# An encoder layer on one core: the first shift-and-scale block summed on TensorE, x and that block loaded first, sixteen feature tiles in six chunks

## The chip, the cores and the metric

One core of a Trainium2 chip runs the whole layer. The metric is device microseconds of one execution; a profiled execution is a separate one with its own time. The profile names five engines and their queues: PE (TensorE), PEld (its weight loads), DVE (VectorE), ACT (ScalarE), POOL (GpSimd), SP (the queue that issues nearly all loads here).

## What is computed

A residual block of width 2048 on 512 tokens. Before any matmul of the token mixer can run, its input `h` has to be normed and modulated by a shift and a scale that come out of a matrix-vector product with 4096 columns of `w_mod`:

```python
cond = jax.nn.silu(c)
mod = (cond @ w_mod[layer] + b_mod[layer]).astype(x.dtype)
shift_a, scale_a, gate_a, shift_m, scale_m, gate_m = [
    m[:, None, :] for m in jnp.split(mod, N_MOD, axis=-1)]
h = _rmsnorm(x, pre_mix_g[layer]) * (1.0 + scale_a) + shift_a
proj = h @ w_in[layer]
```

Attention, a bidirectional gated recurrence, the output projection and the MLP follow; the change touches none of them.

## The kernel before, in words

The 2048 features are 16 **feature tiles** of 128 (`kt`, 0 to 15). Every fp32 product of `h` and a weight is made of three matmuls (`mm3`, lines 227 to 230): high part by high part, and two cross terms. The high part `wH` of a weight chunk is cast on ACT (line 214), the low part `wL` subtracted on DVE (line 215).

The **front stage** (lines 572 to 650) makes `h` for all 16 tiles and, while it does, multiplies them by the four first groups of `w_in`. It takes the tiles in **chunks**, `bounds = [0, 2, 4, 8, 12, 16]`: tiles 0-1, 2-3, 4-7, 8-11, 12-15. For a chunk it needs:

1. the **block** of shift and scale columns of these tiles (`mod_block`, lines 249 to 278): row 16p + k of `w_mod` lies on partition p, and step k of 16 multiplies the block's columns by `cond[:, k]` on DVE and adds them into `modacc` (line 269 the first step, line 271 the other 15). The pieces arrive as tile `mraw`, 512 KB each, two steps of a two-tile block or one of a four-tile block. `to_cols` (lines 280 to 300) then sums over the partitions with one-column matmuls against `ones` on PE (line 295, `modc`), and three small DVE operations make the columns `hb` and `hs`. A block of two tiles has 512 columns, one of four 1024;
2. the transposed tile `xT` on PE (line 627 for the first chunk, by a diagonal of the norm factors; line 629 later), `hv` and `hH` on ACT (lines 631, 632), `hL` on POOL (line 633);
3. the weights: `start_block` (lines 388 to 404) multiplies groups `hg`, `qf`, `bi` in PSUM banks `shg`, `sqf`, `sbi`, four banks a group, two of which can be in use at once. In the first chunk ACT copies a finished bank (line 402), in every later one **DVE adds it** to what stands there (line 404), twelve adds a chunk. The fourth group, `res`, stays in four PSUM banks of its own through all chunks.

The blocks are worked one chunk ahead: `pers` says how many steps of the coming block go beside each weight chunk, `interleave` hands them out, `cuts` spreads the steps of the first block between the loads of `x` (line 594). A scheduler orders each engine's instructions by priority (`tc.high_priority(offset=...)`); each engine and the SP queue then run in that fixed order. `mraw` has four buffers, and a load waits on SP until its buffer is free.

Of the kernel before, what the change touches and what calls it, by code (L numbers as in the profile page):

```python
# [20 lines left out]
P = 128  # L21
S = 512
NT = S // P
# [29 lines left out]
def encoder_layer(ctx: ExitStack, tc: tile.TileContext, a, out):  # L53
# [195 lines left out]
    def mod_block(accs, spans, fin, own=None, pri=PRI):  # L249
# [11 lines left out]
        def step(c):  # L261
            def run():
                with tc.high_priority(offset=pri):
                    _, v = load(source(nk * c, nk), nk, w, own)
                    for k in range(nk):
                        kt = nk * c + k
                        if kt == 0:
                            st["acc"] = accs("modacc")
                            nc.vector.tensor_scalar(st["acc"][:, :w], v[:, k, :], cond[:, 0:1], None, ALU.mult)
                        else:  # L270
                            nc.vector.scalar_tensor_tensor(st["acc"][:, :w], v[:, k, :], cond[:, kt:kt + 1],  # L271
                                                           st["acc"][:, :w], ALU.mult, ALU.add)
            return run
# [6 lines left out]
    def to_cols(h_b, h_s, b_b, b_s, g, bank):  # L280
        def fin(acc):
            n = h_b.shape[-1]
            if n == 4 and bank is sdt:
# [36 lines left out]
    with ExitStack() as ph:  # L320
# [67 lines left out]
        def start_block(gid, k0, k1, units, per, tiles):  # L388
            pri = PRI if k0 else 0
# [182 lines left out]
        with pool("start", side="right") as stp:  # L572
# [3 lines left out]
            def mraw():  # L576
                return stp.tile([P, 1024], F32, tag="mraw", name="mraw", bufs=4)

            bounds = [0, 2, 4, 8, 12, 16]
            mod = []  # L580
            for i in range(len(bounds) - 1):
                k0, k1 = bounds[i], bounds[i + 1]
                w = (k1 - k0) * P
                ks = slice(k0, k1)
                mod.append(mod_block(acc_in(hg), [(P * k0, w), (2048 + P * k0, w)],
                                     to_cols(hb[:, ks], hs[:, ks], b_sa[:, ks], b_ca[:, ks], g_mix[:, ks], mmt), mraw,
                                     PRI if i else 0))
            ahead = [u for m in mod[1:] for u in m]
            pers = [3, 4, 2, 2, 0]
            cuts = [2, 3, 4, 6, 8]  # L590
            for u in mod[0][:cuts[0]]:
                u()
            for t in range(NT):
                nc.sync.dma_start(xn[:, t, :], x_d[t * P:(t + 1) * P, :])
# [23 lines left out]
            res = [banks["mm"].tile([P, 512], F32, tag="res", name=f"res{t}", bufs=4) for t in range(NT)]  # L618
            for i in range(len(bounds) - 1):
# [15 lines left out]
                for gid in order:  # L635
                    start_block(gid, k0, k1, ahead, per, tiles)
                for kt in range(k0, k1, 2):
# [702 lines left out]
```

## Time and profile before

| | us |
|---|---|
| runs of the kernel before | 2435.24, 2437.25, 2430.69 (median 2435.24) |
| the profiled execution's own time | 2436.67 |
| its span, first to last instruction | 2434.8 |
| PE busy, share of the span | 2345.1, 96% |
| DVE busy, share of the span | 1784.1, 73% |

The span is what the trace can be read against; 1.9 us of the execution lie outside it. The shares are means over the whole layer. The front stage is its first tenth and is read by itself, from the timeline and from windows of it; a bracket at the end of a timeline row is the idle time just before it and what ended it.

### The profile page before, as it was taken

The numbers are of one execution on the slowest core, as the hardware profiler recorded it, in microseconds if no ns is written. First come the engines' busy times: TensorE is split into PE (matmuls) and PEld (weight loads), VectorE is DVE, ScalarE is ACT, GpSimd is POOL, SyncE is SP. The second block draws the span as 40 slices with busy tenths as digits, with TensorE's granted clock in tenths as the row PEclk, the third lists the DMA queues.
The fourth block names the chain that finished last, engine by engine and source line by source line (L and its number), as shares of the span: only waits on it lengthen the run. The fifth ranks groups of instructions, "written<-read, shape, count | busy, mean of one in ns | idle before, by whom it ended". The sixth has DMA issues, their size and how long they took to land.

```text
span 2434.8 us, 29654 instructions
## 1 busy us (share of the span) xinstructions
PE 2345.1 (96%) x11342; PEld 1943.7 (80%) x11342; DVE 1784.1 (73%) x2222; ACT 932.9 (38%) x1439; POOL 120.9 (5%) x127
## 2 busy tenths in 40 slices
PE   4999999999999999999999999899999999999998
PEld 3778888888977777779888788778888888888886
DVE  6984776767867667487688888676786678677777
ACT  5223334343454432275533333333333233333342
POOL 0111212121110000000000000000000000000000
PEclk9999999999999999999999999999999999999999
DMA  9873353535531158475345354343333332333234
GB/s 316 288 243 96 113 174 96 173 98 176 184 89 35 35 173 264 150 251 182 121 151 168 114 185 143 107 121 96 118 95 104 92 119 88 109 95 113 87 119 132
DMA packets 193801, 341.77 MB, mean 140 GB/s; under 512 B 16886, under 2 KB 65148, under 8 KB 192124
## 3 DMA queue, kind: packets, MB, share of 16 engines
q1 hardware_dynamic: 192464, 339.72, 44.1%
q8 instruction: 89, 1.46, 0.2%
q14 instruction: 52, 0.43, 0.1%
q10 hardware_dynamic: 1196, 0.16, 0.1%
HBM read 331.45 MB, written 8.39 MB: 140 GB/s over the span
## 4 chain that ended last, share of the span: by engine, by line
PE 62%; DMA 4%; DVE 3%; ACT 1%; issue 1%; DVEq 0%; ACTq 0%; SPq 0%
PE up L230 9%; PE up L228 9%; PE up L229 9%; PE dn L1180 8%; PE dn L1182 8%; PE dn L1181 8%; DMA raw<-in_w_mod_dram 3%; PE wo L229 1%; PE wo L230 1%; PE wo L228 1%; DVE modacc L271 1%; PE upl L230 1%; PE upl L229 1%; PE upl L228 1%; DMA modbg<-in_b_mod_dram 1%; PE sc L880 1%
## 5 line engine op out<-in xcount | busy, mean ns | idle before, releaser
L233 ACT CAST wH<-B 128x1024 fp32r<-128x1024 f32 x210 | 221.2, 1053 | 508.6 <-PE up L229 198.2
L234 DVE TENSOR_TENSOR wL<-B,wH 128x1024 fp32r<-128x1024 f32 x210 | 256.5, 1222 | 175.9 <-PE dn L1181 65.0
L1180 PE MATMUL dn<-wH,fH 128*128 128x512 f32 x840 | 330.2, 393 | 9.2 <-DVE G L1046 7.7
L1182 PE MATMUL dn<-wH,fL 128*128 128x512 f32 x840 | 328.0, 390 | 0.0
L1181 PE MATMUL dn<-wL,fH 128*128 128x512 f32 x840 | 327.3, 390 | 0.0
L214 ACT CAST wH<-raw 128x512 fp32r<-128x512 f32 (+1 forms) x320 | 181.9, 612 | 360.2 <-PE wo L230 57.8
L215 DVE TENSOR_TENSOR wL<-raw,wH 128x512 fp32r<-128x512 f32 (+1 forms) x320 | 220.2, 721 | 91.4 <-issue 49.4
L271 DVE SCALAR_TENSOR_TENSOR modacc<-raw,cond,modacc 128x1024 f32<-128x1024 f32 x120 | 159.3, 1328 | 85.8 <-DMA raw<-in_w_mod_dram 85.1
L230 PE MATMUL up<-recH,wL 128*128 128x512 f32 (+1 forms) x544 | 207.9, 382 | 0.0
L228 PE MATMUL up<-recH,wH 128*128 128x512 f32 (+1 forms) x544 | 207.9, 382 | 0.0
L230 PE MATMUL up<-atH,wL 128*128 128x512 f32 (+1 forms) x544 | 204.6, 379 | 3.0 <-DVE wL L215 3.0
L229 PE MATMUL up<-recL,wH 128*128 128x512 f32 (+1 forms) x544 | 207.3, 381 | 0.0
L228 PE MATMUL up<-atH,wH 128*128 128x512 f32 (+1 forms) x544 | 205.5, 378 | 0.0
L229 PE MATMUL up<-atL,wH 128*128 128x512 f32 (+1 forms) x544 | 205.3, 378 | 0.0
L234 DVE TENSOR_TENSOR wL<-raw,wH 128x1024 fp32r<-128x1024 f32 x120 | 146.4, 1220 | 73.9 <-issue 46.5
L1180 PEld LDWEIGHTS dn<-wH,fH 128*128 128x128 f32 x840 | 158.0, 188 | 45.7 <-DVE G L1046 7.8
L233 ACT CAST wH<-raw 128x1024 fp32r<-128x1024 f32 x120 | 126.4, 1054 | 163.4 <-PE dn L1182 145.5
L1182 PEld LDWEIGHTS dn<-wH,fL 128*128 128x128 f32 x840 | 158.0, 188 | 34.7
L1181 PEld LDWEIGHTS dn<-wL,fH 128*128 128x128 f32 x840 | 158.2, 188 | 33.4 <-DVE B L1149 0.2
L1191 DVE TENSOR_TENSOR y<-y,dn 128x1024 f32<-128x1024 f32 x142 | 172.2, 1213 | 1.1 <-PE dn L1182 1.0
L230 PEld LDWEIGHTS up<-atH,wL 128*128 128x128 f32 x544 | 102.6, 190 | 22.2 <-DVE wL L215 3.2
L230 PEld LDWEIGHTS up<-recH,wL 128*128 128x128 f32 x544 | 102.0, 188 | 22.2
(369 smaller groups left out, 4665.9 us busy)
## 6 DMA issues: line engine op xcount, KB each, us to landing
raw<-in_w_up_dram SPq DMA_DIRECT2D x136, 512.0 KB, 3.8
raw<-in_w_mod_dram SPq DMA_DIRECT2D x128, 512.0 KB, 4.1
B<-in_w_down_dram SPq DMA_DIRECT2D x120, 512.0 KB, 4.2
raw<-in_w_in_dram SPq DMA_DIRECT2D x128, 256.0 KB, 3.1
mraw<-in_w_mod_dram SPq DMA_DIRECT2D x48, 512.0 KB, 5.1
raw<-in_w_out_dram SPq DMA_DIRECT2D x40, 512.0 KB, 4.3
raw<-in_w_in_dram SPq DMA_DIRECT2D x24, 512.0 KB, 5.0
mraw<-in_w_mod_dram SPq DMA_DIRECT2D x32, 256.0 KB, 3.9
```

Of the source, the lines that this page charges most:

```text
L214: nc.scalar.copy(H[:, o], raw[:, o])
L215: nc.vector.tensor_tensor(L[:, o], raw[:, o], H[:, o].bitcast(F32), ALU.subtract)
L228: nc.tensor.matmul(o, s_h, m_h, start=first, stop=False)
L229: nc.tensor.matmul(o, s_h, m_l, start=False, stop=False)
L230: nc.tensor.matmul(o, s_l, m_h, start=False, stop=last)
L233: nc.scalar.copy(h_out, src)
L234: nc.vector.tensor_tensor(l_out, src, h_out.bitcast(F32), ALU.subtract)
L271: nc.vector.scalar_tensor_tensor(st["acc"][:, :w], v[:, k, :], cond[:, kt:kt + 1], st["acc"][:, :w], ALU.mult, ALU.add)
L1180: nc.tensor.matmul(o, sh, mh, start=first, stop=False, skip_group_check=skip)
L1181: nc.tensor.matmul(o, sh, ml_, start=False, stop=False, skip_group_check=skip)
L1182: nc.tensor.matmul(o, sl, mh, start=False, stop=last, skip_group_check=skip)
L1191: nc.vector.tensor_tensor(dst, dst, Xv, ALU.add)
```

## The change

`mod_block` takes a `bank`: with one, every step is four one-column matmuls on PE that sum the pieces straight into a PSUM tile `modp`, and `to_cols` reads its sums there, without `modacc`, `ones` and line 295. Only the first block (`BY_PE = 1`) goes that way, in a bank of the `res` tag. Its loads and those of `x` get priority 400. `mraw` has six buffers for four, the chunk of tiles 4-7 becomes 4-5 and 6-7, `pers` and `cuts` follow, and the first chunk's weights get the priority of the others (`pri = PRI`).

```diff
--- before.py
+++ after.py
@@ -246,7 +246,7 @@
     def acc_in(p):
         return lambda name: p.tile([P, 1024], F32, tag="modacc", name=name, bufs=2)
 
-    def mod_block(accs, spans, fin, own=None, pri=PRI):
+    def mod_block(accs, spans, fin, own=None, pri=PRI, bank=None):
         st = {}
         w = sum(n for _, n in spans)
         nk = 1024 // w
@@ -262,9 +262,15 @@
             def run():
                 with tc.high_priority(offset=pri):
                     _, v = load(source(nk * c, nk), nk, w, own)
+                    if bank and c == 0:
+                        st["acc"] = bank("modp")
                     for k in range(nk):
                         kt = nk * c + k
-                        if kt == 0:
+                        if bank:
+                            for j in range(w // P):
+                                nc.tensor.matmul(st["acc"][:, j:j + 1], v[:, k, j * P:(j + 1) * P], cond[:, kt:kt + 1],
+                                                 start=kt == 0 and j == 0, stop=kt == KD - 1 and j == w // P - 1)
+                        elif kt == 0:
                             st["acc"] = accs("modacc")
                             nc.vector.tensor_scalar(st["acc"][:, :w], v[:, k, :], cond[:, 0:1], None, ALU.mult)
                         else:
@@ -280,7 +286,9 @@
     def to_cols(h_b, h_s, b_b, b_s, g, bank):
         def fin(acc):
             n = h_b.shape[-1]
-            if n == 4 and bank is sdt:
+            if bank is None:
+                sums = [acc[:, 0:n], acc[:, n:2 * n]]
+            elif n == 4 and bank is sdt:
                 sums = []
                 for o in (0, 4):
                     ps = bank("modt")
@@ -386,7 +394,7 @@
             return pss
 
         def start_block(gid, k0, k1, units, per, tiles):
-            pri = PRI if k0 else 0
+            pri = PRI
             hl_ = []
             for kt in range(k0, k1, 2):
                 pcs, w = group_pieces(gid, kt, 2)
@@ -574,24 +582,30 @@
             diag = stp.tile([P, NT, P], F32, name="diag")
             ss = small.tile([P, NT], F32, tag="ssl", name="ssx")
             def mraw():
-                return stp.tile([P, 1024], F32, tag="mraw", name="mraw", bufs=4)
-
-            bounds = [0, 2, 4, 8, 12, 16]
+                return stp.tile([P, 1024], F32, tag="mraw", name="mraw", bufs=6)
+
+            def rest(name):
+                return banks["mm"].tile([P, 512], F32, tag="res", name=name, bufs=4)
+
+            bounds = [0, 2, 4, 6, 8, 12, 16]
             mod = []
+            BY_PE = 1
             for i in range(len(bounds) - 1):
                 k0, k1 = bounds[i], bounds[i + 1]
                 w = (k1 - k0) * P
                 ks = slice(k0, k1)
                 mod.append(mod_block(acc_in(hg), [(P * k0, w), (2048 + P * k0, w)],
-                                     to_cols(hb[:, ks], hs[:, ks], b_sa[:, ks], b_ca[:, ks], g_mix[:, ks], mmt), mraw,
-                                     PRI if i else 0))
+                                     to_cols(hb[:, ks], hs[:, ks], b_sa[:, ks], b_ca[:, ks], g_mix[:, ks],
+                                             None if i < BY_PE else mmt), mraw,
+                                     PRI if i else 400, rest if i < BY_PE else None))
             ahead = [u for m in mod[1:] for u in m]
-            pers = [3, 4, 2, 2, 0]
-            cuts = [2, 3, 4, 6, 8]
+            pers = [3, 3, 3, 4, 3, 0]
+            cuts = [1, 2, 3, 4, 8]
             for u in mod[0][:cuts[0]]:
                 u()
             for t in range(NT):
-                nc.sync.dma_start(xn[:, t, :], x_d[t * P:(t + 1) * P, :])
+                with tc.high_priority(offset=400):
+                    nc.sync.dma_start(xn[:, t, :], x_d[t * P:(t + 1) * P, :])
                 for u in mod[0][cuts[t]:cuts[t + 1]]:
                     u()
             for u in mod[0][8:]:
@@ -615,7 +629,7 @@
             g1 = hg.tile([P, NT, 512], F32, tag="gate", name="gate", bufs=2)
             gt_t[1] = g1
             order = [("hg", 0), ("qf", 0), ("bi", 0)]
-            res = [banks["mm"].tile([P, 512], F32, tag="res", name=f"res{t}", bufs=4) for t in range(NT)]
+            res = []
             for i in range(len(bounds) - 1):
                 k0, k1 = bounds[i], bounds[i + 1]
                 with tc.high_priority(offset=PRI):
@@ -634,6 +648,7 @@
                 per = pers[i]
                 for gid in order:
                     start_block(gid, k0, k1, ahead, per, tiles)
+                res = res or [rest(f"res{t}") for t in range(NT)]
                 for kt in range(k0, k1, 2):
                     pcs, w = group_pieces(("hg", 1), kt, 2)
                     H, L = chunk(pcs, 2, w)
```

In the orders below a row is an instruction or a run of like ones (xN), in program order of its engine; the line numbers of the changed kernel are its own (271 is the new matmul, 275 and 277 the DVE steps, 412 the adds).

PE at the very start of the changed kernel (`modp` are the new sums, `xT` the transposed first tiles, `shg` the first weight group):

```order
L271 MATMUL modp_131<-cond_84,mraw_128 128x1 x2
L126 MATMUL ps_st1_109<-ident_73,st1_100 128x96
L641 MATMUL xT_247<-diag_126,xn_125 128x128
L641 MATMUL xT_256<-diag_126,xn_125 128x128
L641 MATMUL xT_247<-diag_126,xn_125 128x128
L641 MATMUL xT_256<-diag_126,xn_125 128x128
L271 MATMUL modp_131<-cond_84,mraw_128 128x1 x6
L271 MATMUL modp_131<-cond_84,mraw_141 128x1 x8
L271 MATMUL modp_131<-cond_84,mraw_153 128x1 x8
```

64 `modp` products stand on PE where the kernel before has 4 products of line 295; four products on `diag` stand ahead of all but the first two, and four more (not shown) behind the 48th.

DVE at the start, before:

```order
L269 TENSOR_SCALAR modacc<-mraw,cond 128x512
L271 SCALAR_TENSOR_TENSOR modacc<-mraw,cond,modacc 128x512 x5
L238 RECIPROCAL ssx<-ssx 128x2
L271 SCALAR_TENSOR_TENSOR modacc<-mraw,cond,modacc 128x512 x4
L238 RECIPROCAL ssx<-ssx 128x2
L271 SCALAR_TENSOR_TENSOR modacc<-mraw,cond,modacc 128x512 x6
L297 TENSOR_TENSOR hb<-modc,cols 128x2
L298 TENSOR_TENSOR hs<-modc,cols 128x2
L269 TENSOR_SCALAR modacc<-mraw,cond 128x512
```

and now:

```order
L238 RECIPROCAL ssx<-ssx 128x2 x2
L215 TENSOR_TENSOR wL<-raw,wH 128x512 x2
L305 TENSOR_TENSOR hb<-modp,cols 128x2
L306 TENSOR_TENSOR hs<-modp,cols 128x2
L307 SCALAR_TENSOR_TENSOR hs<-hs,cols 128x2
L275 TENSOR_SCALAR modacc<-mraw,cond 128x512
L277 SCALAR_TENSOR_TENSOR modacc<-mraw,cond,modacc 128x512 x5
```

The 16 DVE steps of the first block are gone; the first step of the second block stands behind the sums of the first in both.

DVE in the chunk of tiles 6-7 of the changed kernel (`gate`, `q`, `z`, `v` are the adds, 128x1024 the steps of the block of tiles 8-11):

```order
L277 SCALAR_TENSOR_TENSOR modacc<-mraw,cond,modacc 128x1024
L412 TENSOR_TENSOR gate<-gate,shg_1016 128x512
L412 TENSOR_TENSOR gate<-gate,shg_1024 128x512
L277 SCALAR_TENSOR_TENSOR modacc<-mraw,cond,modacc 128x1024
L412 TENSOR_TENSOR gate<-gate,shg_1032 128x512
L277 SCALAR_TENSOR_TENSOR modacc<-mraw,cond,modacc 128x1024
L412 TENSOR_TENSOR gate<-gate,shg_1040 128x512
L277 SCALAR_TENSOR_TENSOR modacc<-mraw,cond,modacc 128x1024
```

This chunk's adds are new as a set of twelve: before, tiles 4-7 shared one set.

## Rows read from the trace of the kernel before

**Rows 1.** Windows of DVE, columns: stretch, length, busy (count), granted clock, DMA, GB/s:

```profile
32.09:156.74 124.65, 111.18 (x130) 0.97 0.88 295
156.74:200.30 43.56, 25.20 (x36) 0.97 0.48 144
```

**Rows 2.** Timeline of the start, columns: start, duration, engine, line, operation, tiles:

```profile
6.75 1.91 ACT L601 ACTIVATE hL<-xn 128x2048 fp32r<-128x2048 f32 x1 [2.15 <-DMA xn<-in_x_dram]
...
13.09 1.91 ACT L601 ACTIVATE hL<-xn 128x2048 fp32r<-128x2048 f32 x1 [4.33 <-DMA xn<-in_x_dram]
...
17.00 0.69 ACT L606 ACTIVATE diag<-ident,ssx 128x128 f32<-128x128 f32 x2 [0.29 <-DVE ssx L238]
17.45 2.08 PE L627 MATMUL xT<-diag,xn 128*128 128x128 f32 x8 [9.58 <-ACT diag L606]
...
25.39 0.69 ACT L606 ACTIVATE diag<-ident,ssx 128x128 f32<-128x128 f32 x2 [0.23 <-DVE ssx L238]
...
30.04 1.87 PE L295 MATMUL modc<-ones,modacc 128*128 128x1 f32 x8 [2.12 <-DVE modacc L271]
...
32.09 0.48 DVE L269 TENSOR_SCALAR modacc<-mraw,cond 128x512 f32<-128x512 f32 x1
...
41.56 1.14 ACT L214 CAST wH<-raw 128x512 fp32r<-128x512 f32 x2 [6.36 <-DMA raw<-in_w_in_dram]
...
42.23 0.80 PE L228 MATMUL shg<-wH,hH 128*128 128x512 f32 x1 [6.70 <-ACT wH L214]
```

**Rows 3.** Timeline of weight loads and PE, passes at either clock level:

```profile
30.04 1.78 PEld L295 LDWEIGHTS modc<-ones,modacc 128*128 128x128 f32 x8 [2.42 <-DVE modacc L271]
...
45.09 0.63 PE L229 MATMUL shg<-wL,hH 128*128 128x512 f32 x1
45.52 0.63 PE L230 MATMUL shg<-wH,hL 128*128 128x512 f32 x1
...
47.09 0.39 PE L228 MATMUL shg<-wH,hH 128*128 128x512 f32 x1
47.32 0.39 PE L229 MATMUL shg<-wL,hH 128*128 128x512 f32 x1
...
88.73 1.84 PE L295 MATMUL modc<-ones,modacc 128*128 128x1 f32 x16
```

**Rows 4.** Timeline of DVE, the steps, the low parts and the adds:

```profile
25.30 4.69 DVE L271 SCALAR_TENSOR_TENSOR modacc<-mraw,cond,modacc 128x512 f32<-128x512 f32 x6
...
47.56 1.29 DVE L215 TENSOR_TENSOR wL<-raw,wH 128x512 fp32r<-128x512 f32 x2 [0.33 <-ACT wH L214]
...
66.70 2.59 DVE L271 SCALAR_TENSOR_TENSOR modacc<-mraw,cond,modacc 128x1024 f32<-128x1024 f32 x2
...
70.19 1.28 DVE L271 SCALAR_TENSOR_TENSOR modacc<-mraw,cond,modacc 128x1024 f32<-128x1024 f32 x1
71.38 0.68 DVE L404 TENSOR_TENSOR gate<-gate,shg 128x512 f32<-128x512 f32 x1
...
76.82 1.28 DVE L404 TENSOR_TENSOR q<-q,sqf 128x512 f32<-128x512 f32 x2
```

**Rows 5.** Who DVE waited for between 32.09 and 156.74, columns: us in total, times, longest:

```profile
DVE hb L297 <- PE modc L295: 3.7, 3, 2.0
DVE gate L404 <- PE shg L230: 2.8, 3, 1.7
```

**Rows 6.** Timeline around the first bank of tiles 8-11 and of tiles 12-15:

```profile
155.08 0.50 PE L229 MATMUL shg<-wL,hH 128*128 128x512 f32 x1 [2.84 <-DVE wL L215]
...
156.74 0.68 DVE L404 TENSOR_TENSOR gate<-gate,shg 128x512 f32<-128x512 f32 x1
...
160.86 0.69 DVE L404 TENSOR_TENSOR gate<-gate,shg 128x512 f32<-128x512 f32 x1 [2.25 <-PE shg L230]
...
202.82 0.39 PE L228 MATMUL shg<-wH,hH 128*128 128x512 f32 x1
```

**Rows 7.** Window of PE from its first weight matmul, columns as in rows 1:

```profile
42.23:156.74 114.51, 106.47 (x517) 0.97 0.88 296
```

## The prediction

> **What bounds the kernel now.** The page's engine shares (table above) come first: PE is busy 96% of the span, so outside the front stage time moves only with PE's own work, which is the same in both kernels from the last chunk of tiles on. The question is when that chunk starts. Its first matmul stands at 202.82 us [rows 6].
>
> The windows of DVE come next. From 32.09, its first step for the second block, to 156.74, its first add for tiles 8-11, DVE is busy 111.18 of 124.65 us; from there to 200.3 it is busy 25.20 of 43.56 [rows 1]. So up to 156.74 DVE carries nearly all of the time, and after it PE does. I call 156.74 the **milestone**: DVE works in program order, so every step, low part and add ahead of that add has to be done first, and PE can be at most two banks ahead of it. PE's wait just before it, 2.84 us, is for a low part of DVE [rows 6].
>
> The start is read from the timeline [rows 2]. The second pair of norm diagonals is there at 25.39, the sums of the first block begin on PE at 30.04, DVE is free for the second block at 32.09; the first weight matmul starts only at 42.23 because its weights were loaded behind pieces of the second block (cast at 41.56, after 6.36 us of waiting for the load).
>
> **The change, part by part.**
>
> *x first.* x now stands behind one piece of the block instead of between many. The second quarter of x had 3.4 MB loaded up to its end and was used at 13.09; the first had 1.3 MB and was used at 6.75 [rows 2]. It now has 2.36 MB, so by a straight line about 9.9. From the second square to the first diagonal took 3.9 us (13.09 to 17.00): 13.8 now; the second diagonal stands behind one more square (1.91 and its read-out of 0.19), 16.2. Nothing of this is on the path by itself. It matters because PE's order puts four diagonal products ahead of the 3rd `modp` product, so the sums really begin at about 17.3.
>
> *Block one on PE.* A product is two passes in the trace: the four of line 295 show as x8. Eight passes took 1.87 us at 30.04, sixteen took 1.84 us at 88.73 [rows 3], so 0.47 us a product at the lower clock level (1.2 GHz) and 0.23 at the higher (2.4). That it is the lower at 30.04 is told by the 512-column passes: they start every 0.43 us at 45.09 and every 0.23 at 47.09 [rows 3]; the record of the granted clock only begins at 47. A one-column product is nearly all weight load: eight loads took 1.78 of the 1.87 us [rows 3]. (The Trainium skill, "TensorE: Matmul & The Clock Gate", section "LDWEIGHTS (loading the stationary operand)", gives a load columns divided by 1.2 in ns, so 0.107 us for 128 whatever the columns moved; as an estimate the 128 loads would cost 13.7 us. The row has 0.22 for each of these fp32 loads, twice that, and it decides; on the point that a single moved column pays for a whole load the trace agrees.)
>
> 64 products cost 30 us at the lower level, 15 at the higher. PE idles for most of the time before 42.23, so nobody has seen whether a run of such products raises the clock. I take that it rises after some 4.5 us of unbroken work, as it did between 42.23 and 47 [rows 2, 3]: 4.5 us from 17.3 do 10 of the 46 products ahead of the next diagonal pair, 36 more take 8.4, four diagonal products 1.0 (half of 2.08 [rows 2]), the last 16 take 3.7. That ends at 34.9, with `hb` out at 35.1 and DVE free for block two at **35.3 against 32.09, 3.2 us later**. The end not taken is the first rival's, 48.8. What went away, 16 DVE steps of 0.78 us (six in 4.69 [rows 4]), lay where DVE was waiting for loads, and frees nothing later, because block two still stands behind the sums in DVE's order.
>
> *First matmul.* `hH` follows `hs` by some 2 us, as before, and the weights are already cast. The first weight matmul comes at about 37.3 instead of 42.23. That is 5 us gained on PE. It is only kept if PE is the bound, and by rows 1 it is not.
>
> *Six chunks.* I counted DVE's operations from the start of block two to the milestone in both orders. Steps of 512 columns: 45 for 15, at 0.78: +23.4. Steps of 1024: 27 for 39, at 1.25 (1.30 each where two follow one another, 1.19 to the start of the next operation where an add follows [rows 4]): -15.0. First steps of a block, three of 512 and two of 1024 for one and three: +0.2. Adds: 36 for 24, two in 1.28 [rows 4]: +7.7. Low parts: 34 for 36, two in 1.29: -1.3. That is +15.0. Two thirds of the new 512-steps alternate with other work, where a 1024-step was 0.11 us cheaper; this takes off 2: **+13.0**, between 11 and 15. Part of it, three steps, is work for tiles 12-15 done earlier than before; that helps nobody, as PE bounds afterwards.
>
> *DVE's idle time.* 13.5 us lay idle before the milestone [rows 1], most of it waits for PE: 3.7 for the sums of a block and 2.8 for `gate` banks lead the list [rows 5]. With more to do and PE ahead of it, DVE waits less. I leave 4.5 us: waits for the four block sums (one of them was up to 2.0 us [rows 5]) and for the weights of the first chunk. **-9.0**; the ends are -13.5 and -4.
>
> *Behind the milestone.* Before, PE had finished one bank of tiles 8-11 at 156.74; the second add came at 160.86, 2.25 us of it waited for [rows 6]. From the milestone to the last chunk's first matmul it took 46.1 us. When DVE is late, PE stands two banks ahead: twelve passes, 2.7 us less. **-2.5**.
>
> *Six mraw buffers, priorities, pers, cuts.* Priced at nothing by themselves. The DMA share up to the milestone is 0.88 [rows 1], and in the changed order loads wait for DVE to free `mraw`, so more buffers can't go faster than DVE. If that cover were gone, loads would bound instead, at 295 GB/s: the 45 MB of x, weights and pieces ahead of the milestone need 153 us, still under the time DVE needs.
>
> **Sum.** 3.2 + 13.0 - 9.0 - 2.5 = +4.7 us on 2436.67, the profiled execution: 2441.4. The runs shown have a median of 2435.24, 1.4 lower, which would give 2440; I write **2441**. With the ends of the terms this case runs from 2431 to 2450. A measurement of this kernel can tell about 0.3%, 7.3 us, from no change.
>
> **The rivals.**
>
> *The sums stay at the lower clock level.* For it: every short burst on PE before 42.23 ran at that level, and a one-column product moves almost nothing. Against: PE works without a break from 17.3 on, which none of those bursts did. Then 46 products take 21.5, four diagonals 2.1, sixteen 7.5: the sums end at 48.4 and DVE begins block two at 48.8, 16.7 us late. DVE idles 2 us less, loads having run ahead. 16.7 + 13.0 - 11.0 - 2.5 = +16.2: 2452 to 2453, clearly slower, and the first matmul comes at about 50.
>
> *DVE does keep up, and the time falls.* The price is PE's: 5 us at the start, and what of 8.0 us idle (114.51 less 106.47 [rows 7]) and some 4 us at the lower clock up to the milestone goes. Up to -17, 2420. It decides if DVE's work per two-tile chunk stays under PE's 23 us (96 passes of 0.23 and the transposes). Sixteen steps of 0.7 to 0.78, eight low parts of 0.64 and twelve adds of 0.64 make 24 to 25 us before any disturbance, and 32 in the chunk of tiles 6-7, whose sixteen steps are of 1024 columns. That speaks against it; smoother chunks and less lockstep speak for it.
>
> *The order moves and the time does not:* each late step is made good by idle time. 2435.
>
> **How the numbers follow.** Forecast 0.45, low clock 0.30, DVE keeps up 0.20, nothing moves 0.05. The forecast's 2431 to 2450 puts some 0.4 of it above +7.3 us and nearly all the rest within: slower 0.18 + 0.29 = 0.47; same 0.26 + 0.05 + 0.05 = 0.36; faster 0.17. Of the range, 2427 leaves out most of the fast rival (0.14) and 2457 little of the slow one (0.06).
>
> **What would show it.** The first step of block two on DVE at 35 (forecast) or 48 (rival); `modp` pairs of passes at 0.23 or 0.47; the first weight matmul at 37 or 50; DVE busy over 95% from there to the first add of tiles 8-11, and that add at 162 to 166 instead of 156.74; the last chunk's first matmul near 207.5 instead of 202.82. An add at 150 or earlier with DVE idle in between would make the count of DVE's work the wrong bound and the fast rival right.

## The result and the profile after

The changed kernel takes 2459.9 us (median of 4 runs, 2456.99 to 2463.1); the kernel before, run beside it on the same chip, takes 2433.0 (4 runs, 2429.16 to 2437.25). The ratio is 1.011, 95% interval 1.0098 to 1.0123: slower by some 27 us. The forecast was 2441 with a range up to 2457, so the time lies outside, and the mechanism that decided it is the first rival's, at a larger price than the rival gave.

The profiled execution took 2456.99 us, its span is 2455.2 (before: 2436.67 and 2434.8), so the two profiles differ by 20.4 where the medians differ by 27. The page shows where to look: the PE row gains 26 us of busy time against 2345.1 before, and its first slice of 61 us is now 60% busy where it was 40%.

```profile
span 2455.2 us, 29931 instructions
...
PE 2371.1 (97%) x11462; PEld 1968.4 (80%) x11462; DVE 1775.4 (72%) x2237; ACT 932.6 (38%) x1439; POOL 118.6 (5%) x127
...
PE   6899999999999999999999999999999999999998
```

The timeline of the changed kernel's start, all engines (columns as in [rows 2]):

```profile
14.50 1.91 ACT L615 ACTIVATE hL<-xn 128x2048 fp32r<-128x2048 f32 x1 [5.57 <-DMA xn<-in_x_dram]
...
20.60 0.39 ACT L620 ACTIVATE diag<-ident,ssx 128x128 f32<-128x128 f32 x1
...
24.47 19.79 PE L271 MATMUL modp<-cond,mraw 128*128 128x1 f32 x92 [2.21 <-DMA mraw<-in_w_mod_dram]
...
44.11 2.05 PE L641 MATMUL xT<-diag,xn 128*128 128x128 f32 x8
45.96 6.83 PE L271 MATMUL modp<-cond,mraw 128*128 128x1 f32 x32
...
52.82 0.16 DVE L305 TENSOR_TENSOR hb<-modp,cols 128x2 f32<-128x2 f32 x1 [22.30 <-PE modp L271]
...
53.16 0.48 DVE L275 TENSOR_SCALAR modacc<-mraw,cond 128x512 f32<-128x512 f32 x1
...
55.79 0.77 PE L228 MATMUL shg<-wH,hH 128*128 128x512 f32 x1
...
65.05 0.74 DVE L277 SCALAR_TENSOR_TENSOR modacc<-mraw,cond,modacc 128x512 f32<-128x512 f32 x1
65.71 0.68 DVE L215 TENSOR_TENSOR wL<-raw,wH 128x512 fp32r<-128x512 f32 x1
...
183.73 0.68 DVE L412 TENSOR_TENSOR gate<-gate,shg 128x512 f32<-128x512 f32 x1
```

Read it from the top. The second quarter of x is squared at 14.50, the second diagonal is there at 20.60, and after it PE does 92 passes of one column in 19.79 us: 0.215 us a pass, which is the lower clock level of [rows 3] (eight passes in 1.78 to 1.87). The eight diagonal passes at 44.11 take 2.05, as at 17.45 before [rows 2], and the last 32 passes take 0.213 each. So the level did not rise in 28 us, with PE busy all the time. DVE waits 22.30 us for the sums and begins block two at 53.16, not 32.09 [rows 2]. The first weight matmul comes at 55.79, not 42.23; the milestone, DVE's first add for tiles 8 to 11, at 183.73, not 156.74 [rows 6]: 27.0 us later.

Windows of DVE in the changed kernel, from block two to the milestone and on to the next set of adds (columns as in [rows 1]), and the window of PE over the sums:

```profile
53.16:183.73 130.57, 116.30 (x160) 0.96 0.87 284
183.73:229.80 46.07, 22.41 (x35) 1.00 0.35 103
```

```profile
24.47:52.79 28.32, 28.32 (x132) 1.00 0.39 121
```

The stretch that was 124.65 us long [rows 1] is 130.57: DVE has 5.1 us more work in it and idles 14.3 us where it idled 13.5. PE is busy for all 28.32 us of the sums (the clock column is 1.00 there as everywhere ahead of the record's start, at some 57 us here; the level is told by the length of the passes). The DMA share there is 0.39, since the six `mraw` buffers come free only as PE uses them. The waits of the queue on SP from 25 to 55 us (us in total, times, longest) say so:

```profile
SPq L205 <- PE modp L271: 22.7, 8, 4.7
```

### The profile page after: what moved, and what is told of

The parts are those of the page before. It is cut to its first block, busy times and chain, and to the rows that moved or that the text cites. A ratio compares the mean times of both kernels' runs of the same rounds, so it can differ in the third digit from the quotient of the medians.

```text
span 2455.2 us, 29931 instructions
## 1 busy us (share of the span) xinstructions
PE 2371.1 (97%) x11462; PEld 1968.4 (80%) x11462; DVE 1775.4 (72%) x2237; ACT 932.6 (38%) x1439; POOL 118.6 (5%) x127
## 4 chain that ended last, share of the span: by engine, by line
PE 62%; DMA 4%; DVE 3%; ACT 1%; issue 1%; DVEq 0%; ACTq 0%; SPq 0%
PE up L230 9%; PE up L228 9%; PE up L229 9%; PE dn L1195 8%; PE dn L1197 8%; PE dn L1196 8%; DMA raw<-in_w_mod_dram 2%; PE wo L230 1%; PE wo L229 1%; PE wo L228 1%; DVE modacc L277 1%; PE upl L230 1%; PE upl L229 1%; PE upl L228 1%; PE pT L913 1%
```

## The experiments

Two theories were set against each other first. **A**: the 21 us by which DVE starts block two later are the loss, and the sixth chunk with its adds is worth little. **B**: the sixth chunk with its adds is the loss. What each run gave stands in one table. Its columns are: DVE's first step of block two; PE's first weight matmul; the first add for tiles 8 to 11; PE's first product of the stage behind the sixteen tiles (`gqf`); and the ratio of the times with its interval. Each ratio is to the kernel before on the same chip, whose median was 2428 to 2433 us in every comparison; the trace of before is that of the sections above.

| kernel | block two | first weight matmul | add, tiles 8-11 | next stage | ratio |
|---|---|---|---|---|---|
| before | 32.09 | 42.23 | 156.74 | 246.9 | 1 |
| changed | 53.16 | 55.79 | 183.73 | 271.7 | 1.0110 (1.0098 to 1.0123) |
| six_chunks_dve_sums | 34.08 | 48.58 | 164.94 | 252.6 | 1.0046 (1.0029 to 1.0063) |
| five_chunks_pe_sums | 53.11 | 55.74 | 178.43 | 268.3 | 1.0115 (1.0100 to 1.0130) |
| five_chunks_dve_sums | 34.84 | 49.34 | 160.72 | 250.0 | 1.0026 (1.0015 to 1.0037) |
| sums_128_columns | 38.21 | 45.07 | 165.22 | 254.8 | 1.0056 (1.0041 to 1.0071) |
| half_steps | 32.03 | 42.93 | 148.40 | 237.2 | 0.9964 (0.9951 to 0.9977) |
| hl_on_dve | 31.94 | 42.28 | 154.61 | 243.7 | 0.9996 (0.9987 to 1.0005) |
| act_ends_block_one | 57.66 | 59.29 | 186.48 | 274.4 | 1.0064 (1.0048 to 1.0079) |
| pe_held | 31.79 | 60.77 | 173.63 | 264.1 | 1.0075 (1.0060 to 1.0091) |
| dve_held | 32.88 | 43.63 | 173.25 | 263.3 | 1.0065 (1.0052 to 1.0079) |
| dve_held_8_buffers | 29.37 | 41.53 | 173.19 | 260.8 | 1.0058 (1.0044 to 1.0071) |
| block_two_starts_early | 44.15 | 58.1 | 183.89 | 271.9 | 1.0102 (1.0089 to 1.0116) |
| const_moved_32_bytes | 34.65 | 45.27 | 158.00 | 247.3 | 0.9955 (0.9943 to 0.9968) |
| weights_moved_64_bytes | 31.85 | 42.4 | 157.07 | 246.3 | 1.0003 (0.9993 to 1.0012) |
| rec_moved_32_bytes | 32.09 | 42.65 | 158.16 | 248.4 | 0.9951 (0.9938 to 0.9965) |

The last three have the instruction order of the kernel before in this stage, and their next stage starts at 246.3 to 248.4: about 2 us either way are scatter of single traces.

### The parts of the change, apart

Three kernels undo one or two parts; in all of them x stays first, and the six buffers and the new priorities stay.

```
six_chunks_dve_sums:   BY_PE = 0
five_chunks_pe_sums:   bounds = [0, 2, 4, 8, 12, 16]; pers = [3, 4, 2, 2, 0]
five_chunks_dve_sums:  both
```

> The change without its sums on TensorE: six chunks, x first and the new buffers stay, DVE sums the first block as before. Theory A (the 21 us by which the sums on PE delay DVE's second block are the loss, and the extra chunk is worth the 5 us of added DVE work): 2 to 8 us slower than before, 2435 to 2441; DVE's first step of block two at 33 to 37, its first add for tiles 8-11 at 160 to 167. Theory B (the extra chunk with its twelve adds is the loss, a late start would be made good from DVE's idle time): at least 15 us slower than before, 2448 or more.

> The change with the five chunks of before; sums on TensorE, x first and six buffers stay. Theory A: 15 to 22 us slower than before, 2448 to 2455, with DVE's first step of block two at 52 to 54. Theory B: under 8 us slower than before, the same late first step notwithstanding.

> Only the load order is left of the change: x and the first block first, first weights at the priority of the others, six buffers; five chunks, DVE sums. Theory A: the first weight matmul at 36 to 39 instead of 42, DVE's block two at 33 to 37, and the time within 5 us of before, since DVE sets the pace up to tiles 8-11. Theory B: the same. If the load order itself were the loss, it would be over 10 us slower.

The sums on PE decide. With them on DVE the six chunks cost 1.0046, with five chunks and the sums on PE the whole loss is there, 1.0115. B is out. At the next stage's start the load order alone stands 3.1 us late, six chunks with it 5.7, the sums on PE 21.4 with five chunks and 24.8 with six. The times say nearly the same, except that they tell no difference between six and five chunks with the sums on PE, and are 2 to 5 us above the traces in these rows; that rest is open. Theory A had both losses too small: six chunks cost 8.7 us in the medians where it said 2 to 8, five chunks with the sums on PE 26.8 where it said 15 to 22.

The load order was not free, and its expectation (first weight matmul at 36 to 39) failed: 49.34. In this kernel DVE's order puts steps of block two ahead of the last of block one's, and PE waits 15 us for the end of the sums (timeline of PE in five_chunks_dve_sums):

```profile
43.93 1.87 PE L303 MATMUL modc<-ones,modacc 128*128 128x1 f32 x8 [15.11 <-DVE modacc L277]
```

### Is it the single moved column?

The same 64 products, with `cond`'s column broadcast to 128 equal columns as the moving operand; the sums are read from every 128th column of the bank (lines shortened).

```
-  matmul(acc[:, j:j + 1], v[:, k, ...], cond[:, kt:kt + 1], ...)
+  matmul(acc[:, j * P:(j + 1) * P], v[:, k, ...], cond[:, kt:kt + 1].broadcast_to([P, P]), ...)
```

> The changed kernel, its sums with a moving operand of 128 equal columns instead of one; the same 64 products, weights and order, and sums read from every 128th column. If the one moved column is what keeps the clock at its lower level: passes at 0.26 us at first, then 0.13, DVE's block two at 39 to 44 instead of 53, and 8 to 14 us faster than the changed kernel, 2446 to 2452. If the clock stays low for any run of such products behind loads: passes at 0.26 throughout, block two at 57 to 60, 4 to 7 us slower than the changed kernel, 2463 to 2467.

Timeline and windows of PE in this run:

```profile
24.54 15.83 PE L271 MATMUL modp<-cond,mraw 128*128 128x128 f32 x124 [2.20 <-DMA mraw<-in_w_mod_dram]
40.22 1.05 PE L642 MATMUL xT<-diag,xn 128*128 128x128 f32 x8
...
45.07 0.66 PE L228 MATMUL shg<-wH,hH 128*128 128x512 f32 x1
```

```profile
24.54:27.50 2.96, 2.96 (x14) 1.00 0.91 298
...
30.00:40.20 10.20, 10.20 (x93) 1.00 0.92 291
```

Fourteen passes in 2.96 us are 0.211 each, 93 in 10.20 are 0.110: here the level rises early in the run of products, and the eight diagonal passes take 1.05 instead of 2.05. With the same products, the same start and 128 times the moved columns, the 124 passes take 15.83 us where the changed kernel's 92 and 32 take 26.62. These 10.8 us are what the level costs by itself. DVE has `hb` at 42.55 instead of 52.82 and the first weight matmul comes 10.7 us earlier.

The gain further on is larger: the next stage comes at 254.8 instead of 271.7 and the ratio falls from 1.011 to 1.0056, two thirds of the loss in the trace and half of it in the times. (The expectation had longer passes, 0.26 and 0.13 us, and a gain of 8 to 14 us; the medians give 15.) That larger part is not the clock's alone, because the orders of this kernel differ too: DVE does a third low part and six steps of block two ahead of `hb`, PE does the second four diagonal products behind all the sums, and weights are loaded earlier. No run parts the two. (By the Trainium skill, "TensorE: Matmul & The Clock Gate", section "LDWEIGHTS (loading the stationary operand)", a load of 128 columns takes 0.107 us; the 0.110 a pass at the higher level agrees, the 0.215 at the lower one is twice that.)

### What passes the delay on

The prediction said that DVE's own work sets the pace up to the milestone. Two kernels lighten DVE in the kernel before. half_steps leaves out half of the products of the later blocks' sums.

```
half_steps:  wd = w // 2 if own and pri else w      # for every step but each block's first
hl_on_dve:   nc.vector.tensor_tensor(hL[:, kt, :], hv, hH[:, kt, :].bitcast(F32), ALU.subtract)   # was nc.gpsimd
```

> The kernel before, in which every VectorE step of the later blocks' sums but each block's first works on half of its columns; half of those products are left out, so this times less VectorE work and is not the same result. It asks what sets the pace between the first step of block two and the first add of tiles 8 to 11 (124.65 us in the kernel before, 125.3 to 130.9 in every version so far, whenever it begins). If VectorE's own work sets it (theory A needs this, since a late start is then passed on in full), the 80 or so steps there lose some 25 to 30 us, the add comes at least 12 us earlier than 156.74, and the time falls by 8 to 16 us. If the loads set it (DMA share 0.88 in that stretch), the add moves by under 4 us and the time by under 3.

> The kernel before, in which the subtraction that gives hL of a later tile group is made by VectorE instead of GpSimd. In the kernel before such an operation takes GpSimd about 1.5 to 1.9 us and the VectorE operation beside it is drawn out by about 1 us; on VectorE it costs about 0.6. If VectorE's work sets the pace up to the first add of tiles 8 to 11, the stretch falls from 124.65 to about 119 and the time by 3 to 6 us; if the loads do, the stretch moves by under 2 us and the time by nothing that can be measured.

The window of DVE in half_steps from block two to the milestone:

```profile
32.03:148.40 116.37, 82.88 (x130) 1.00 0.90 307
```

Against [rows 1] DVE has 28.3 us less work and the stretch is 8.3 us shorter; the other 20 us turn into idle time (13.5 before, 33.5 now). For the milestone neither side of the expectation holds (12 us or more, or under 4), while the time fell by 8.7 us, within the first side's 8 to 16: DVE's work is a part of the pace, not the pace.

Taking GpSimd's subtractions away moved the milestone by 2.1 us and the time by nothing that can be told. But it shortened DVE's operations. In this kernel DVE makes the twelve subtractions itself (8.0 us) and is still busy for 2.4 us less, 108.76 for 111.18 [rows 1], because its steps and low parts take less without GpSimd beside them. The groups of DVE in hl_on_dve from block two to the milestone (mean ns of one behind the comma; the same groups of before stand in the part on the prediction):

```profile
L271 DVE SCALAR_TENSOR_TENSOR modacc<-mraw,cond,modacc 128x1024 f32<-128x1024 f32 x41 | 52.4, 1279 | 0.7 <-DMA mraw<-in_w_mod_dram 0.4
L215 DVE TENSOR_TENSOR wL<-raw,wH 128x512 fp32r<-128x512 f32 x36 | 23.8, 685 | 3.8 <-ACT wH L214 2.2 <-PE sbi L229 0.7 <-PE shg L229 0.5
L271 DVE SCALAR_TENSOR_TENSOR modacc<-mraw,cond,modacc 128x512 f32<-128x512 f32 x15 | 11.3, 750 | 0.4
```

The next kernel was to start DVE early and leave PE late: ScalarE (ACT) adds block one's constants, and `mraw` has eight buffers (the line for `hb`; that for `hs` is left out here).

```
-  nc.vector.tensor_tensor(h_b, sums[0], b_b, ALU.add)
+  nc.scalar.activation(h_b[:, j:j + 1], acc[:, j:j + 1], AF.Identity, bias=b_b[:, j:j + 1])
```

> The changed kernel, in which ScalarE, not VectorE, adds the constants to block one's sums, so that VectorE's steps for block two do not stand behind TensorE's 64 products; two more buffers for the blocks' loads, or else these would wait instead. TensorE's first weight matmul still comes at about 55 us. Theory A (the loss is VectorE's late start): block two's first step comes at 26 to 36 us, the first add of tiles 8 to 11 at 158 to 170, and the time is 12 to 20 us below the changed kernel's, 2440 to 2448. Rival (the loss is TensorE's late first matmul): the add stays within 4 us of 183.7 and the time within 5 us of the changed kernel's. Between the two: both count, and the add's place gives the shares.

It did not do what it was built for. The first casts of `wH` now stood behind the sums on ACT, and DVE's order has the low parts `wL` of these weights ahead of block two (timeline of ACT and DVE in this run):

```profile
55.01 0.26 ACT L293 ACTIVATE hb<-modp,cols 128x1 f32<-128x1 f32 x1 [24.76 <-PE modp L273]
...
55.78 1.15 ACT L216 CAST wH<-raw 128x512 fp32r<-128x512 f32 x2
```

```profile
56.45 1.29 DVE L217 TENSOR_TENSOR wL<-raw,wH 128x512 fp32r<-128x512 f32 x2 [31.62 <-ACT wH L216]
57.66 0.48 DVE L277 TENSOR_SCALAR modacc<-mraw,cond 128x512 f32<-128x512 f32 x1
```

DVE started 4.5 us later than in the changed kernel, and the next stage 2.7 us later. So it doesn't decide between the two theories. Yet the time was 1.0064, some 11 us better. Most of that gain lies behind 1100 us and has another cause; it has a part of its own below.

Then either engine was held by itself for 21 us, in the kernel before, by work that nobody reads.

```
pe_held:   51 products matmul(idle[:, 0:1], ident, hs[:, 0:1]) ahead of the first chunk's transposes
dve_held:  28 operations tensor_scalar(idle, xn[:, 0, 0:1024], hs[:, 0:1], ALU.mult) behind block one
dve_held_8_buffers:  the same, mraw with bufs=8 instead of 4
```

> The kernel before with 51 useless products of one column (102 passes) put on TensorE behind block one's shift and scale and ahead of the transposes of the first chunk, so that TensorE is held from about 32 to 54 us while VectorE's sums and all loads go on as before. First weight matmul at 54 to 57 us instead of 42.23. If VectorE with its loads sets the pace (theory A): block two's first step stays at 32, the first add of tiles 8 to 11 comes at 156 to 162, the time is up by 0 to 5 us. If TensorE's late first matmul is what the changed kernel lost: the add comes 10 to 14 us later, at 167 to 171, and the time is up by 8 to 15.

> The kernel before with 28 useless operations of 128x1024 (0.75 us each, 21 us) put on VectorE right after block one's shift and scale, ahead of nearly all of block two's steps. The sums stay on VectorE and the chunks are five. Theory A: the first add of tiles 8 to 11 comes 17 to 21 us later, at 174 to 178, as with the sums on TensorE (178.43 with five chunks), and the time is up by 13 to 21. If the sums on TensorE cost something else (the clock, TensorE's own late start), this stays under half of that.

> The same hold of VectorE with eight buffers for the blocks' loads instead of four, so that 2 MB more can land during the hold. If VectorE's own work is the pace after the hold, the add stays within 3 us of the run with four buffers. If the loads are (they stand still while VectorE holds their buffers), it comes 5 to 8 us earlier and the time with it.

Held DVE gives what A wanted, 16.4 us at the next stage and 1.0065 in time. But held PE, with DVE's sums and first step where they were, gives as much: 17.2 us and 1.0075. A, as it was put, fails here. (The first weight matmul came at 60.77, not 54 to 57, and the add at 173.63 is later than either side of that expectation had it.) The timeline of pe_held shows why the two holds are one:

```profile
33.19 21.92 PE L613 MATMUL idle<-hs,ident 128*128 128x1 f32 x102 [1.52 <-DVE hs L299]
...
57.06 0.78 ACT L635 ACTIVATE hv<-xT,hb,hs 128x512 f32<-128x512 f32 x1 [27.86 <-PE xT L631]
...
60.10 1.13 ACT L214 CAST wH<-raw 128x512 fp32r<-128x512 f32 x2
...
60.75 1.95 DVE L215 TENSOR_TENSOR wL<-raw,wH 128x512 fp32r<-128x512 f32 x2 [18.89 <-ACT wH L214]
```

PE is late with the transposes, ACT stands 27.86 us at `hv`, its cast of the next weights stands behind `hv`, and DVE, after twelve steps of block two, stands 18.89 us at the `wL` that needs the cast. DVE ran on for some 10 us and was then stopped like the rest. In dve_held it goes the other way round: PE had two matmuls out at 43.63 and its next at 56.02, because their `wL` stood behind the hold (timeline of PE in dve_held):

```profile
43.63 1.22 PE L228 MATMUL shg<-wH,hH 128*128 128x512 f32 x2 [7.32 <-ACT wH L214]
56.02 0.80 PE L229 MATMUL shg<-wL,hH 128*128 128x512 f32 x1 [11.16 <-DVE wL L215]
```

Eight buffers let more land (281 GB/s from 25 to 55 us for 171), and the milestone moved by 0.06 us; the next stage is 2.5 us earlier, about the scatter. This does not rule the loads out: DVE's order differs in that kernel, and its hold stood from 39.62 to 60.28, with steps of block two ahead of it, where with four buffers it stood from 34.05 to 54.69.

One more run asked whether an early DVE helps at all when the others are late: the changed kernel with ACT ending block one, this time tied to the first `wL`, so that the casts come first. `mraw` has eight buffers again; the line that makes the tie is:

```
+  nc.vector.scalar_tensor_tensor(bs, pre[0][1][:, 1, 510:512].bitcast(F32), 0.0, b_sa[:, 0:2], ALU.mult, ALU.add)   # bs: the bias of h_b
```

> The changed kernel, in which ScalarE adds the constants to block one's sums, after its casts of the first weights, so that VectorE's first eight steps of block two (some 6 us of work) stand ahead of the end of TensorE's 64 products and no longer behind it; eight buffers for the blocks' loads. What follows these steps on VectorE is the second weights' wL, which waits for a cast that stands behind the sums on ScalarE. If VectorE's late start by itself is the loss: first step at 28 to 36 us, the first add of tiles 8 to 11 at 165 to 172, the time 10 to 17 us below the changed kernel's. If the loss is the stop of the whole chain of wH, wL and TensorE, of which VectorE's start is only a part: the add comes by no more than those 6 us earlier, at 177 to 184, and the time falls by 0 to 6 us (ratio to the kernel before 1.008 to 1.011).

The timeline of DVE in this run:

```profile
44.15 0.49 DVE L278 TENSOR_SCALAR modacc<-mraw,cond 128x512 f32<-128x512 f32 x1 [11.59 <-DMA mraw<-in_w_mod_dram]
...
65.33 0.69 DVE L218 TENSOR_TENSOR wL<-raw,wH 128x512 fp32r<-128x512 f32 x1 [8.66 <-ACT wH L217]
...
183.89 0.68 DVE L421 TENSOR_TENSOR gate<-gate,shg 128x512 f32<-128x512 f32 x1
```

Block two begins at 44.15, 9 us earlier than in the changed kernel (not at 28 to 36: its loads stand behind the pieces that PE had not used yet). Six of its eight steps are done before the sums end, the last two at 56.7, and DVE then waits 8.66 us at the next `wL`, which it reaches at 65.33; in the changed kernel the same `wL` ran at 64.44. The milestone is 183.89 against 183.73, the ratio 1.0102. So DVE's start by itself was not the loss. What these runs leave as the reading is that PE, ACT, DVE and the loads stop together until the sums end, and go on from there in lockstep; how much of it the loads carry by themselves was not parted off.

### A gain from 32 bytes

Most of the 11 us of act_ends_block_one came in one kind of product: those of `up` with `recH` and `recL` take 560.7 us there where they take 569.2 before. One of the three groups of PE in five kernels (before, act_ends_block_one up to 2378 us, const_moved_32_bytes, weights_moved_64_bytes, rec_moved_32_bytes; columns: line, engine, operation, tiles, count, busy us, mean ns of one):

```profile
L228 PE MATMUL up<-recH,wH 128*128 128x512 f32 x480 | 190.0, 396 | 0.0
```

```profile
L230 PE MATMUL up<-recH,wH 128*128 128x512 f32 x478 | 186.1, 389 | 0.0
```

```profile
L229 PE MATMUL up<-recH,wH 128*128 128x512 f32 x480 | 186.7, 389 | 0.0
```

```profile
L229 PE MATMUL up<-recH,wH 128*128 128x512 f32 x480 | 190.0, 396 | 0.0
```

```profile
L228 PE MATMUL up<-recH,wH 128*128 128x512 f32 x480 | 186.7, 389 | 0.0
```

In act_ends_block_one a small constant had moved every tile behind it by 32 bytes, `wH` and `wL` too, while `recH` and `recL`, counted from the other end of the memory, stayed. Three kernels put an unused tile in the kernel before.

```
const_moved_32_bytes:    pad = const.tile([P, 8], F32)     # ahead of hs
weights_moved_64_bytes:  pad = const.tile([P, 16], F32)    # ahead of hs
rec_moved_32_bytes:      pad = recp.tile([P, 8], F32)      # behind recL
```

> The kernel before with an unused tile of 32 bytes a partition among the constants, and nothing else; every tile allocated after it moves by 32 bytes. In the run act_ends_block_one the products of the second half of the up projection took 389 ns where they take 395 to 396 in all others, and its weight tiles lay 32 bytes further on, the tiles recH and recL where they were. If the place of the weight tiles against recH and recL is what did it, those 1440 products fall to 389 here too and the time by 7 to 10 us (2418 to 2421 beside 2428 on the same chip); if it was something else in that run, nothing changes (within 2 us).

> As const_moved_32_bytes, with 64 bytes in place of 32. There the products of up with recH and recL took 389 ns instead of 395, and the weight tiles stood at the same address modulo 64 as recH and recL (32 and 32), where in the kernel before they stand at 0 and 32. With 64 bytes they stand at 0 and 32 again. If that is what counts: 395 to 396 ns again and the time of the kernel before within 4 us. If any move helps: 389 ns and a time 8 us or more below.

> The kernel before with the unused 32 bytes put beside recH and recL, so that these two move and the weights stay: 0 and 0 modulo 64. If the two addresses must agree modulo 64: 389 ns and the time 7 to 12 us below the kernel before. If the weights' own place is what counts: 395 ns and no change. The gain of const_moved_32_bytes in time (12 us) is more than its 1440 faster products give (about 9); whatever is missing here belongs to other tiles that moved there.

The addresses modulo 64 that the build gives the weights and `rec` are 0 and 32 before and with 64 bytes (396 ns), 32 and 32 with the constant moved, 0 and 0 with `rec` moved (389 ns). Where they agree, the 1440 products take 560.1 us instead of 569.2, and the 384 products of `wo` with `rec` 1.4 to 1.7 us less. That is 10.5 us or a little more of the 11 to 12 us by which the times fall: 2415.97 and 2417.68 beside 2427.99 and 2428.98. Both beat the kernel before and the changed one, with the old order of every engine in place. In block_two_starts_early two small constants move the weights by 64 bytes, and these products take 396 ns again.

## Why the prediction was wrong

Its sum was made at the last chunk's first matmul: forecast +4.7, measured 226.98 against 202.82 [rows 6], +24.2. The measured terms are +21.1 for DVE's start, +5.1 for its work, +0.8 for its idle time and -2.8 behind the milestone, which add up. They are an account of DVE's time up to the milestone and not yet causes: the experiments show that DVE's start alone does not pass the delay on.

**The step that failed** is "I take that it rises after some 4.5 us of unbroken work". The rows from which that was read, 42.23 to 47, are of 512-column products; products of one column had not been seen in a long run. The passes stayed at the lower level from 24.47 to 52.79, with PE busy throughout [rows 3 give the two levels]. DVE began block two at 53.16 instead of 35.3, which is 17.9 us. Of these, 10.7 are the level (from the first product behind the diagonals to the last, 28.3 us and not 17.6), and 7.2 are the later start of the sums. The whole sum is off by 19.5; the terms for six chunks and for idle time miss by -7.9 and +9.8 and nearly cancel, which is chance. The first weight matmul, forecast for 37.3, came at 55.79.

**x first** was placed too early as well. The straight line through bytes loaded gave 9.9 for the second quarter; it was used at 14.50, and the sums began at 24.47, not 17.3. By 14.50 some 4.4 MB had come (301 GB/s from 0 on) where the straight line counted 2.36: 2 MB of other loads had run beside those of x. Another 2.21 us went to a wait for a piece of the block. So the first rival, which had the mechanism right, had its start wrong: it let DVE begin at 48.8, not 53.16. Its price for a product at the lower level, 0.47 us, was too high (two passes, 0.43). It lost 16.2 where 24.2 were lost: 4.4 of these 8 us are the start, the rest is the idle time (-11.0 there, +0.8 measured) less what it had too much for the chunks (13.0, measured 5.1).

**Six chunks**, +13.0, measured +5.1 in the busy time of DVE. The counts held (45 steps of 512, 27 of 1024, 34 low parts, 36 adds); the durations did not. A 512-step that alternates with a low part takes 0.66 from start to start (65.05 to 65.71 above), not the 0.78 of six in a row [rows 4]; for such gains the sum had taken off 2 us. And DVE's operations were drawn out, more before the change than after it. The groups of DVE in the stretch up to the milestone, first before, then after (mean ns of one behind the comma):

```profile
L271 DVE SCALAR_TENSOR_TENSOR modacc<-mraw,cond,modacc 128x1024 f32<-128x1024 f32 x39 | 54.7, 1402 | 1.3 <-DMA mraw<-in_w_mod_dram 0.9
L215 DVE TENSOR_TENSOR wL<-raw,wH 128x512 fp32r<-128x512 f32 x36 | 28.6, 820 | 3.0 <-ACT wH L214 1.3 <-DMA mraw<-in_w_mod_dram 0.7 <-issue 0.4
L271 DVE SCALAR_TENSOR_TENSOR modacc<-mraw,cond,modacc 128x512 f32<-128x512 f32 x15 | 13.0, 869 | 0.5
```

```profile
L277 DVE SCALAR_TENSOR_TENSOR modacc<-mraw,cond,modacc 128x512 f32<-128x512 f32 x45 | 37.5, 837 | 0.4
L277 DVE SCALAR_TENSOR_TENSOR modacc<-mraw,cond,modacc 128x1024 f32<-128x1024 f32 x27 | 35.5, 1315 | 0.0
L215 DVE TENSOR_TENSOR wL<-raw,wH 128x512 fp32r<-128x512 f32 x34 | 24.1, 716 | 7.5 <-ACT wH L214 5.1 <-DMA mraw<-in_w_mod_dram 2.4
```

Large steps averaged 1.40 us before and 1.32 after, low parts 0.82 and 0.72. hl_on_dve shows what draws them out: without GpSimd's subtractions these groups average 1.28 and 0.69, and the 512-steps 0.75 for 0.87. Against these means the three groups were drawn out by an estimated 11 us before and 6 after, from the counts and means shown. So 5 to 6 of the 7.9 us by which the term missed are work that GpSimd no longer drew out; the rest was not taken apart.

**DVE's idle time**, -9.0, measured +0.8. This term rested on "up to 156.74 DVE carries nearly all of the time", and half_steps shows that this reading of [rows 1] was wrong: busy for 111 of 124.65 us, DVE still gave back only 8.3 us when 28.3 were taken away. In the changed kernel 5.06 us of its idle time are one wait for `wH` at 64.44, behind the late restart. With the sums on DVE the two terms come nearer: the stretch of six_chunks_dve_sums is 130.86 long with 121.49 busy, work +10.3 and idle -4.1.

**Behind the milestone**, -2.5, measured -2.8 (43.25 to the last chunk's first matmul instead of 46.08).

**Buffers, priorities, pers, cuts**, priced at nothing: the load order with them costs about 3 us at the next stage and 1.0026 in time, through DVE's order, which lets block two pass the end of block one.

The signs for which the text told the reader to look (block two at 48, passes of a pair at 0.47, first matmul at 50) picked out the right case. Its chance was 0.30, because that every short burst before 42.23 ran at that level was set against the unbroken work, and only the second of these was new.

## What to carry to other kernels

A run of one-column products that begins at the lower clock level should be priced at it to its end, unless a trace shows otherwise; here only those that stood among wide products ran at the higher one (sixteen passes in 1.84 us at 88.73 [rows 3]). A delay at the head of a pipeline of in-order queues was not absorbed here by engines that could have run ahead, because each soon met an item that needed the late one: look in each queue for the first such item before counting on slack, and remove work from an engine in an experiment before calling it the bound. Before the durations of one engine's operations are priced, see what another engine does beside them. When a variant moves the time in a stage that it doesn't touch, compare the mean duration of the same products and the addresses of their tiles.

## What the runs showed of the hardware

28 us of unbroken one-column fp32 products (with eight passes of 128 columns among them) ran at 0.215 us a pass and stayed at the lower level to their end; the same products with 128 moved columns ran at 0.211 for the first 14 passes and at 0.110 for most of what followed. In pe_held 102 other one-column passes took 21.92 us, 0.215 each, again without a rise.

With GpSimd's twelve subtractions in the stretch, DVE's steps of 128x1024 averaged 1.40 us and its low parts 0.82; with them on DVE 1.28 and 0.69. The adds, 0.68 in both, were not drawn out.

A product of 128x512 took 395 to 396 ns where the address of the `rec` tile modulo 64 differed from that of the weights by 32, and 389 where it did not, in both of the ways in which they can agree. Why was not looked into; one size and one kind of number was seen.
